# A three-layer transformer on one core: the order of issue found by alternating forward and backward list schedules, and two modulation rows spread by a transpose on TensorE

## The chip, the cores and the metric

The kernel runs on one core of one Trainium2 chip. Its time is the device time of one execution in microseconds (us). The median of the runs is compared before and after the change.

## What is computed

Input is x of 512 tokens by 1024 features, all in float32. A first block has two layers. Each computes a modulation from a condition vector, mixes the tokens, and adds a gated, normalised result:

```python
cond = jax.nn.silu(c)
for layer in range(DEPTH):
    mod = cond @ w_ada[layer] + b_ada[layer]
    shift, scale, gate = jnp.split(mod, 3, axis=-1)
    h = rmsnorm(x, g_pre[layer]) * (1.0 + scale[:, None, :]) + shift[:, None, :]
    ...
    x = x + gate[:, None, :] * rmsnorm(y, g_post[layer])
```

Layer 1's mixer has attention in a sliding window with sinks (8 heads) beside latent attention (8 heads, "MLA"). Layer 2's has differential attention (4 heads) beside forgetting attention (8 heads). In both the concatenated heads are multiplied by `silu` of a gate and go through an output projection w_out. Then follows a second block: one layer with native sparse attention, stick-breaking attention and a gated linear recurrence, an output projection and a layer norm. The output is 512 by 1024.

## The kernel before, in words

**Tiling.** Weights come as tiles of 128 x 1024 float32 (512 KB). Each tile is split into a high part, a rounded copy by ScalarE (L109, `whir<-wrawr`), and a low part, a subtraction on VectorE or POOL (L113, `wlor`). Activations are split likewise (`hh` and `hl`, L90 and L95). A product then takes three matmuls, high by high, high by low and low by high (`mm3`, L80), so that the result is exact to about float32.

**Stages.** The program is written out once, with no loops on the chip. In time: loads and layer 1's first modulation and normalised input (0 to about 62 us), layer 1's input projection and window attention (to about 200), its latent attention (to about 290), the output projection, residual and layer 2's normalised input (to about 350), layer 2 (to about 600), the second block (to about 950) and its output projection with the layer norm.

**Modulation.** `cond @ w_ada` is done on VectorE. Eight tiles of w_ada are loaded (L157, into `graw`, a single buffer; at the start into other free tiles, `V`) and summed up, each times one column of cond: L175 starts and L177 continues the sum `sa`. A matmul with ones over the partitions then makes columns of it (`gemv_cols`, L179 to 186, result `modc`) or a row for the gate (`gate_row`, L205 to 218). Layer 1's rows are needed at once; those of layer 2 and both gates are computed beside layer 1's attention. Layer 1's scaled input is `hh` by ScalarE (L684) and `hl` by VectorE (L690), from `moda` (L682).

**Layer 2's scale and shift** are columns of 128 x 8 and are wanted as rows on all partitions. `spread` (L252 to 258) writes a column to DRAM with its two axes exchanged and reads it back as a row of 1024 on 128 partitions (tag `pth`). The rows are used in `hgen` (L239, L241), which makes layer 2's input of each block of 128 tokens in `residual` (L588 to 623).

**Attention.** Scores `sr` come from TensorE; a custom instruction of VectorE masks them and takes their maximum (L383, `nm`); ScalarE exponentiates (L385); POOL multiplies by the reciprocal sum (L395, `Pr`); TensorE transposes (L140, `tr`); ScalarE and VectorE split the transposed probabilities (`pthr` L90, `ptl` L95); TensorE multiplies by V (`o`). Rotary sums are L316 to L327. The gate's SILU (`gates`, L524 and L526) is one ScalarE instruction over 128 x 2048 between two loads of function tables.

**Order of issue.** All DMAs are issued by SP. Each engine takes its instructions in a fixed order, which a planner (`Plan`, L1784 on) sets when the program is built. It collects dependencies (`edges`): hard ones, ones from the reuse of buffers ("room") and soft ones. `schedule` is a list schedule forward in time over a model of costs (durations, a bus and eight lanes for DMAs, the slower clock of TensorE behind idle time); at each step the engine takes the ready instruction of the lowest rank. The rank is 84% the place in the program and 16% the longest path to the end. `pin` sorts by the modelled start and ties each engine's instructions to that order.

## Time and profile before

| | |
|---|---|
| three runs | 988.75, 992.36, 995.62 us (median 992.36) |
| profiled execution, its own time | 997.87 us |
| its span, first to last instruction | 996.1 us |
| mean granted clock of TensorE | 0.977 |
| busy: TensorE, VectorE, ScalarE, POOL | 919.3, 711.8, 536.0, 245.6 us |
| moved by DMA | 137.38 MB |

TensorE (PE in rows) is busy for 92% of the span, VectorE (DVE) for 71%, ScalarE (ACT) for 54%. A granted clock of 1.00 is 2.4 GHz and 0.50 is 1.2 GHz; TensorE's matmuls then take about twice as long. Busy shares hide which stage an engine waits in, so the profile is to be read by stages and by waits: an idle time in brackets stands behind the instruction that came after it, with what it waited for. PEld is TensorE's weight load.

### The profile page before, as it was taken

The page shows a single profiled execution, that of the slowest core. Times are in us where ns is not written, and L with a number is a line of the kernel's source. Part 1 is how long each engine was busy: PE and PEld are TensorE (multiplying, and loading weights), DVE is VectorE, ACT ScalarE, POOL GpSimd, SP SyncE. Part 2 cuts the span into 40 slices and gives each one's busy share as a digit, 9 for nine tenths or more (in the row PEclk, how much of TensorE's full clock was granted, in tenths as well). Part 3 has the DMA queues.
Part 4 walks back from the last instruction along what each step waited for, and adds up shares of the span by engine and source line. Part 5 has one row for each costly group of instructions (what it writes and reads, how often), then busy time and mean ns, then how long its engine had stood idle before and what let it go on. Part 6 is the DMA issues. An engine that isn't in the chain of part 4 may idle for free.

```text
span 996.1 us, 14786 instructions
## 1 busy us (share of the span) xinstructions
PE 919.3 (92%) x4999; PEld 765.5 (77%) x4999; DVE 711.8 (71%) x1581; ACT 536.0 (54%) x1180; POOL 245.6 (25%) x274
## 2 busy tenths in 40 slices
PE   2899899788799898999999999999999999999996
PEld 1688787666678787879888878986888887888775
DVE  6767768866788954876455856467589788787748
ACT  5543665736654443657345864365254386676820
POOL 1230032202331001322011221014134334544440
PEclk9899999798999999999999999998999999999998
DMA  9637645356565646661454634243422433431142
GB/s 358 258 94 208 206 106 145 101 138 157 160 187 171 199 149 170 174 179 42 124 148 120 189 124 130 87 142 103 135 85 69 106 92 97 128 95 44 49 163 85
DMA packets 56671, 137.38 MB, mean 138 GB/s; under 512 B 15047, under 2 KB 15431, under 8 KB 56596
## 3 DMA queue, kind: packets, MB, share of 16 engines
q1 hardware_dynamic: 56596, 136.44, 46.7%
q8 instruction: 40, 0.66, 0.3%
q14 instruction: 35, 0.29, 0.1%
HBM read 105.42 MB, written 8.44 MB: 114 GB/s over the span
## 4 chain that ended last, share of the span: by engine, by line
PE 44%; DVE 6%; ACT 3%; DMA 2%; issue 1%; POOL 1%; DVEq 0%; ACTq 0%; SPq 0%; POOLq 0%
PE accr L80 32%; PE sr L80 6%; PE o L80 3%; PE tr L140 2%; DMA wrawr<-in_w_out_dram 1%; DVE wlor L113 1%; DMA qk<-qk 1%; DVE ptl L95 1%; PE tr L80 0%; PE sr L140 0%; DMA wrawr<-in_w_dram 0%; ACT whir L109 0%; DVE graw L1660 0%; DVE tmpr L1635 0%; ACT Pr L385 0%
## 5 line engine op out<-in xcount | busy, mean ns | idle before, releaser
L80 PE MATMUL accr<-hh,whir 128*128 128x512 f32 x516 | 208.3, 407 | 5.0 <-DVE qk L327 4.5
L80 PE MATMUL accr<-hl,whir 128*128 128x512 f32 x516 | 208.1, 405 | 4.8 <-DVE hl L690 4.8
L80 PE MATMUL accr<-hh,wlor 128*128 128x512 f32 x516 | 207.3, 405 | 0.0
L109 ACT CAST whir<-wrawr 128x1024 fp32r<-128x1024 f32 (+5 forms) x110 | 111.5, 1014 | 109.4 <-PE accr L80 72.2
L113 DVE TENSOR_TENSOR wlor<-wrawr,whir 128x1024 fp32r<-128x1024 f32 (+6 forms) x93 | 118.3, 1273 | 63.8 <-ACT whir L109 63.5
L395 POOL TENSOR_SCALAR Pr<-Pr,sm 128x256 f32<-128x256 f32 (+2 forms) x120 | 76.8, 656 | 220.9 <-DVE sm L1154 45.8
L80 PEld LDWEIGHTS accr<-hh,whir 128*128 128x128 f32 x516 | 99.0, 192 | 27.9 <-DVE qk L327 5.3
L80 PE MATMUL accr<-whir,hh 128*128 128x256 f32 (+4 forms) x364 | 116.0, 325 | 2.9 <-DVE hS L95 1.0
L385 ACT ACTIVATE Pr<-Pr,nm 128x256 f32<-128x256 f32 (+3 forms) x176 | 95.7, 545 | 41.6 <-DVE nm L383 40.5
L80 PEld LDWEIGHTS accr<-hl,whir 128*128 128x128 f32 x516 | 98.9, 192 | 23.0 <-DVE hl L690 5.7
L80 PE MATMUL accr<-whir,hl 128*128 128x256 f32 (+4 forms) x364 | 115.0, 324 | 0.4 <-DVE hl L95 0.3
L80 PE MATMUL accr<-wlor,hh 128*128 128x256 f32 (+4 forms) x364 | 114.2, 322 | 0.9 <-DVE wlor L113 0.9
L80 PEld LDWEIGHTS accr<-hh,wlor 128*128 128x128 f32 x516 | 98.9, 192 | 20.5 <-issue 1.8
L80 PE MATMUL sr<-qk,qk 128*128 128x256 f32 (+11 forms) x400 | 95.3, 335 | 11.1 <-DVE nm L383 5.1
L95 DVE TENSOR_TENSOR ptl<-tr,pthr 128x256 fp32r<-128x256 f32 (+3 forms) x160 | 72.4, 464 | 25.0 <-ACT pthr L90 21.5
L80 PEld LDWEIGHTS sr<-qk,qk 128*128 128x128 f32 (+2 forms) x400 | 67.5, 196 | 23.9 <-DVE nm L383 10.4
L140 PE MATMUL tr<-ident,Pr 128*128 128x128 f32 x392 | 75.4, 293 | 11.0 <-DVE ptl L95 5.0
L80 PEld LDWEIGHTS accr<-whir,hh 128*128 128x128 f32 x364 | 69.1, 191 | 8.9 <-DVE hS L95 1.2
L80 PEld LDWEIGHTS accr<-whir,hl 128*128 128x128 f32 x364 | 68.8, 190 | 5.4 <-DVE hl L95 0.9
L80 PEld LDWEIGHTS accr<-wlor,hh 128*128 128x128 f32 x364 | 68.8, 191 | 5.1 <-DVE wlor L113 1.2
L140 PEld LDWEIGHTS tr<-ident,Pr 128*128 128x128 f32 x392 | 49.5, 149 | 27.7 <-issue 9.5
L90 ACT CAST pthr<-tr 128x384 fp32r<-128x384 f32 (+3 forms) x124 | 52.9, 439 | 32.5 <-PE tr L140 31.3
(369 smaller groups left out, 1736.5 us busy)
## 6 DMA issues: line engine op xcount, KB each, us to landing
graw<-in_w_ada_dram SPq DMA_DIRECT2D x32, 512.0 KB
wrawr<-in_w_od_dram SPq DMA_DIRECT2D x30, 512.0 KB
wrawr<-in_w_dram SPq DMA_DIRECT2D x29, 512.0 KB
qk<-qk SPq DMA_DIRECT2D x111, 128.0 KB
wrawr<-in_w_out_dram SPq DMA_DIRECT2D x24, 512.0 KB
wrawr<-in_w_ev_dram SPq DMA_DIRECT2D x17, 512.0 KB
V<-in_w_ada_dram SPq DMA_DIRECT2D x14, 512.0 KB
qk<-tmpr SPq DMA_DIRECT2D x34, 128.0 KB
```

Of the source, the lines that this page charges most:

```text
L80: self.nc.tensor.matmul(out, a, b, start=start, stop=stop, skip_group_check=True)
L90: self.nc.scalar.copy(hi, src)
L95: self.nc.vector.tensor_tensor(lo, src, hi.bitcast(F32), ALU.subtract)
L109: self.nc.scalar.copy(hi[:, :n], raw[:, :n])
L113: eng.tensor_tensor(lo[:, :n], raw[:, :n], hi[:, :n].bitcast(F32), ALU.subtract)
L140: self.nc.tensor.transpose(out, in_, self.ident[:k, :k])
L385: nc.scalar.activation(Pi, Pi, AF.Exp, bias=nm[:, i:i + 1], scale=-1.0, accum_out=s[:, i:i + 1])
L395: self.nc.gpsimd.tensor_scalar(v, v, r[:, i:i + 1], 1.0, ALU.mult, ALU.mult)
```

## The change

Two parts. First, the planner searches. `schedule` is split into `graph` (the dependencies in both directions and the longest paths), `forward` (the list schedule as before, which now also returns the modelled end) and a new `backward` (a list schedule from the end, whose times are the latest starts). `pin` does six rounds: forward by a rank, then backward, whose times are the next rank. Of the six forward schedules the one with the earliest modelled end is kept. The first rank takes 10% of the longest path instead of 16%. That DMAs are now known by their type and not by the issuing engine changes nothing, since SP issues them all.

```diff
-    PATH = 0.16
+    PATH, ROUNDS = 0.10, 6
...
+    def backward(self, rank):
+        n = len(self.ins)
+        need = [len(a) for a in self.after]
+        ready, back = [0.0] * n, [0.0] * n
...
+        for _ in range(n):
+            t, e = min((max(free[e], 0.0 if here[e] else coming[e][0][0]), e) for e in range(5) if here[e] or coming[e])
...
+                heapq.heappush(here[e], (-rank[i] - self.cost[i][1], i))
+            i = heapq.heappop(here[e])[1]
+            back[i], free[e] = t, t + self.cost[i][1]
+            for a, kind in self.before[i]:
+                ready[a] = max(ready[a], free[e] - self.cost[a][1] + (0 if kind else self.whole[a] + self.LATENCY[e]))
...
+        return [-b - c[1] for b, c in zip(back, self.cost)]
...
     def pin(self):
         hard, room, soft = self.edges()
-        start = self.schedule(hard, room, soft)
+        path = self.graph(hard, room, soft)
+        n, top = len(path), max(path)
+        rank = [i / n * (1 - self.PATH) - self.PATH * p / top for i, p in enumerate(path)]
+        tries = []
+        for _ in range(self.ROUNDS):
+            tries.append(self.forward(rank))
+            rank = self.backward(tries[-1][1])
+        start = min(tries)[1]
```

Second, `spread` transposes on the chip. TensorE turns the 128 x 8 column into 8 x 128 in PSUM, ScalarE copies it to the row's tile, and the DMA writes eight lines of 512 bytes. It is called twice.

```diff
     def spread(self, col):
         d = self.dram([8, 128])
-        self.nc.sync.dma_start(d.rearrange("c p -> p c"), col)
+        ps = self.p("o")
+        self.tr(ps[0:8, 0:128], col)
         row = self.t([128, 1024], "pth")
+        self.nc.scalar.copy(row[0:8, 0:128], ps[0:8, 0:128])
+        self.nc.sync.dma_start(d, row[0:8, 0:128])
         self.nc.sync.dma_start(row, d.rearrange("(o c) p -> o (c p)", o=1).to_broadcast([128, 1024]))
```

TensorE gets two instructions more and ScalarE two (the copies), and no other engine gains or loses any. Lines from 256 on move down by three. What moves in the order is shown at three places.

VectorE at the start, before: layer 1's first modulation (`modc`, `moda`), the low halves `hl` of its input, and the sum `sa` for its later columns, with tile `V_71` of w_ada.

```order
L177 SCALAR_TENSOR_TENSOR sa_60_258<-V_65_270,cond_5_72,sa_60_258 128x1024
L690 SCALAR_TENSOR_TENSOR hl_59_239<-qk_42_181,moda_57_237,hh_58_238 128x512
L753 TENSOR_SCALAR nsink_87_477<-sink_86_475 128x8
L177 SCALAR_TENSOR_TENSOR sa_60_258<-V_71_308,cond_5_72,sa_60_258 128x1024
L185 TENSOR_TENSOR modc_56_226<-o_55_225,bada_13_94 128x4
L690 SCALAR_TENSOR_TENSOR hl_59_239<-qk_44_188,moda_57_237,hh_58_238 128x512
L682 SCALAR_TENSOR_TENSOR moda_57_237<-modc_56_226,gpre_12_92 128x4
L690 SCALAR_TENSOR_TENSOR hl_59_239<-qk_46_195,moda_57_237,hh_58_238 128x512
L690 SCALAR_TENSOR_TENSOR hl_59_239<-qk_48_202,moda_57_237,hh_58_238 128x512
```

The same place now.

```order
L177 SCALAR_TENSOR_TENSOR sa_60_258<-V_65_270,cond_5_72,sa_60_258 128x1024
L693 SCALAR_TENSOR_TENSOR hl_59_239<-qk_40_174,moda_57_237,hh_58_238 128x512
L693 SCALAR_TENSOR_TENSOR hl_59_239<-qk_42_181,moda_57_237,hh_58_238 128x512
L693 SCALAR_TENSOR_TENSOR hl_59_239<-qk_44_188,moda_57_237,hh_58_238 128x512
L185 TENSOR_TENSOR modc_56_226<-o_55_225,bada_13_94 128x4
L693 SCALAR_TENSOR_TENSOR hl_59_239<-qk_46_195,moda_57_237,hh_58_238 128x512
L685 SCALAR_TENSOR_TENSOR moda_57_237<-modc_56_226,gpre_12_92 128x4
L177 SCALAR_TENSOR_TENSOR sa_60_258<-V_71_308,cond_5_72,sa_60_258 128x1024
L693 SCALAR_TENSOR_TENSOR hl_59_239<-qk_48_202,moda_57_237,hh_58_238 128x512
```

The sum over `V_71` has gone behind two more `hl`, `modc` and `moda`.

ScalarE in layer 1's window attention, before: `Pr2` and `Pr3` are the probabilities of two heads' blocks, `og_233` half of the gate.

```order
L90 CAST pthr0_346_1683<-tr1_351_1699 128x2x128
L385 ACTIVATE Pr2_353_1705,sm_355_1707<-Pr2_353_1705,nm_354_1706 128x128
L524 ACT_TABLE_LOAD
L524 ACTIVATE og_233_1172<-og_233_1172 128x2048
L526 ACT_TABLE_LOAD
L385 ACTIVATE Pr2_353_1705,sm_355_1707<-Pr2_353_1705,nm_354_1706 128x256 x3
L815 ACTIVATE sk_e_360_1728<-nm_354_1706,sink_86_475 128x4
L435 COPY tmpr2_369_1773<-o_368_1764 64x512
L385 ACTIVATE Pr3_376_1798,sm_378_1800<-Pr3_376_1798,nm_377_1799 128x128
L397 ACTIVATE Pr2_353_1705<-Pr2_353_1705,sm_355_1707 128x128
```

The same engine now, some twenty rows later; the exponentials of `Pr2` and `Pr3` stand ahead of the first of these rows.

```order
L854 ACTIVATE hh_363_1741<-accr0_365_1743,subln_362_1739 128x512
L438 COPY tmpr2_369_1773<-o_368_1764 64x512
L90 CAST pthr1_370_1777<-tr0_374_1788 128x2x128
L90 CAST pthr1_370_1777<-tr1_375_1793 128x2x128
L854 ACTIVATE hh_363_1741<-accr1_366_1750,subln_362_1739 128x512
L854 ACTIVATE hh_363_1741<-accr2_367_1757,subln_362_1739 128x512
L854 ACTIVATE hh_363_1741<-accr0_394_1875,subln_362_1739 128x512
L400 ACTIVATE Pr3_376_1798<-Pr3_376_1798,sm_378_1800 128x128
L527 ACT_TABLE_LOAD
L527 ACTIVATE og_233_1172<-og_233_1172 128x2048
L529 ACT_TABLE_LOAD
L90 CAST pthr0_386_1841<-tr0_388_1843 128x128
```

The SILU with its table loads has gone behind the last instruction on `Pr3`.

VectorE in the latent attention, before: `Pr1_541` is a block of scores, `ptl` the low half of transposed probabilities, `graw_518` a tile of w_ada.

```order
L383 ISA Pr1_541_2508,nm_542_2509<-sr1_545_2517,cm_89_481 128x256
L383 ISA nm_542_2509 128x1
L95 TENSOR_TENSOR ptl_506_2366<-tr1_510_2382,pthr1_505_2365 128x4x128
L962 RECIPROCAL sm_513_2391<-sm_513_2391 128x4
L177 SCALAR_TENSOR_TENSOR sa_435_2087<-graw_518_2421,cond_5_72,sa_435_2087 128x1024
L383 ISA Pr1_541_2508,nm_542_2509<-sr0_546_2523,cm_89_481 128x384
L383 ISA nm_542_2509 128x1
L94 CAST pthr0_521_2436<-tr0_523_2438 128x128
```

The same place now.

```order
L386 ISA Pr1_541_2508,nm_542_2509<-sr1_545_2517,cm_89_481 128x256
L386 ISA nm_542_2509 128x1
L439 TENSOR_TENSOR tmpr4_450_2138<-o_503_2352,tmpr2_504_2361 64x512
L965 RECIPROCAL sm_513_2391<-sm_513_2391 128x4
L386 ISA Pr1_541_2508,nm_542_2509<-sr0_546_2523,cm_89_481 128x384
L386 ISA nm_542_2509 128x1
L95 TENSOR_TENSOR ptl_506_2366<-tr0_509_2376,pthr1_505_2365 128x3x128
L95 TENSOR_TENSOR ptl_506_2366<-tr1_510_2382,pthr1_505_2365 128x4x128
L94 CAST pthr0_521_2436<-tr0_523_2438 128x128
L386 ISA Pr1_541_2508,nm_542_2509<-sr1_547_2529,cm_89_481 128x512
```

The sum over `graw_518` is gone from here and stands 43 rows later; those over `graw_502`, `graw_548`, `graw_564` and `graw_581` have moved back by 35, 42, 38 and 31 rows. On SP the two writes of `spread` stood in layer 1's attention, 95 and 62 rows ahead of their reads; now both writes and both reads stand within five rows, behind the last load of w_out0.

## Rows read from the trace of the kernel before

**Rows 1.** Stages: length; busy us (instructions) of PE, PEld, DVE, ACT, POOL; PEclk; DMA; GB/s.

```profile
0.00:62.00 62.00, 36.48 (x194) 30.33 (x194) 43.97 (x72) 34.52 (x59) 11.83 (x10) 0.94 0.65 248
...
200.00:232.00 32.00, 25.90 (x120) 20.21 (x119) 18.04 (x42) 10.93 (x24) 1.05 (x1) 0.95 0.57 135
232.00:290.00 58.00, 49.25 (x274) 40.10 (x275) 48.67 (x131) 41.90 (x111) 21.22 (x27) 0.94 0.60 166
...
450.00:700.00 250.00, 249.95 (x1312) 209.42 (x1311) 149.18 (x308) 138.66 (x278) 48.08 (x53) 0.99 0.42 123
```

**Rows 2.** TensorE's waits: tile, line, releaser: us in total, times, longest.

```profile
PE sr L140 <- DMA ident<-in_ident_dram: 19.6, 1, 19.6
PE sr L80 <- DVE nm L383: 5.1, 4, 3.3
PE tr L140 <- DVE ptl L95: 5.0, 6, 1.9
...
PE accr L80 <- DVE hl L690: 4.8, 1, 4.8
PE accr L80 <- DVE qk L327: 4.5, 2, 2.9
PE sr L140 <- DVE Pr L241: 4.5, 2, 3.4
```

**Rows 3.** Granted clock in four slow stretches and in the last projection.

```profile
35.20:42.00 6.80, 5.74 (x14) 4.48 (x15) 6.31 (x11) 4.55 (x6) 2.05 (x1) 0.50 0.52 190
...
188.80:195.60 6.80, 6.24 (x27) 5.18 (x27) 5.21 (x11) 4.37 (x13) 2.90 (x5) 0.50 0.27 78
226.30:229.70 3.40, 3.40 (x10) 2.73 (x11) 0.00 (x0) 0.00 (x0) 0.00 (x0) 0.50 0.45 107
243.40:246.80 3.40, 3.16 (x13) 2.61 (x12) 2.83 (x12) 2.72 (x8) 0.43 (x1) 0.50 0.56 116
...
965.55:987.62 22.07, 22.03 (x97) 17.70 (x95) 18.13 (x39) 2.55 (x7) 2.39 (x1) 1.00 0.13 49
```

**Rows 4.** VectorE's timeline at the start: start, duration, line, operation, operands.

```profile
32.38 3.10 DVE L177 SCALAR_TENSOR_TENSOR sa<-V,cond,sa 128x1024 f32<-128x1024 f32 x1 [1.58 <-DMA V<-in_w_ada_dram]
...
36.20 0.74 DVE L690 SCALAR_TENSOR_TENSOR hl<-qk,moda,hh 128x512 fp32r<-128x512 f32 x1
```

**Rows 5.** ScalarE's timeline about the gate's SILU in layer 1.

```profile
179.41 1.28 ACT L524 ACT_TABLE_LOAD   x1
...
183.92 0.51 ACT L385 ACTIVATE Pr<-Pr,nm 128x256 f32<-128x256 f32 x1
```

**Rows 6.** TensorE's timeline behind it; in brackets the idle time before and its releaser.

```profile
187.19 0.55 PE L140 MATMUL tr<-ident,Pr 128*128 128x128 f32 x3 [2.60 <-POOL Pr L395]
```

**Rows 7.** SP's timeline: a w_ada row, the column's write, a later w_ada row.

```profile
207.47 0.33 SPq L157 DMA_DIRECT2D graw<-in_w_ada_dram  x1
208.74 0.38 SPq L255 DMA_DIRECT2D d<-moda  x1
...
236.75 0.58 SPq L157 DMA_DIRECT2D graw<-in_w_ada_dram  x1
```

**Rows 8.** VectorE's timeline: three sums over w_ada rows.

```profile
217.57 1.28 DVE L177 SCALAR_TENSOR_TENSOR sa<-graw,cond,sa 128x1024 f32<-128x1024 f32 x1 [2.86 <-DMA graw<-in_w_ada_dram]
...
241.43 1.28 DVE L177 SCALAR_TENSOR_TENSOR sa<-graw,cond,sa 128x1024 f32<-128x1024 f32 x1 [0.85 <-DMA graw<-in_w_ada_dram]
...
258.18 1.28 DVE L177 SCALAR_TENSOR_TENSOR sa<-graw,cond,sa 128x1024 f32<-128x1024 f32 x1 [3.77 <-DMA graw<-in_w_ada_dram]
```

**Rows 9.** DMA packets from 212 to 219 us.

```profile
DMA packets 503, 0.34 MB, mean 48 GB/s; under 512 B 414, under 2 KB 414, under 8 KB 503
```

**Rows 10.** ScalarE's timeline: the cast of a chunk of w_out0.

```profile
223.19 1.04 ACT L109 CAST whir<-wrawr 128x1024 fp32r<-128x1024 f32 x1 [5.99 <-DMA wrawr<-in_w_out_dram]
```

**Rows 11.** Instructions on the spread rows: durations, first and last start.

```profile
L257 SPq DMA_DIRECT2D pthr<-d x2: 327/327/327, 286.3 to 293.2; - x2
...
L239 DVE SCALAR_TENSOR_TENSOR Pr<-Pr,st_r,pthr x8: 742/748/753, 319.4 to 344.9; 128x512 f32<-128x512 f32 x8
```

More of the change, by code (lines that the diff above doesn't have):

```diff
@@ L1801, in __init__ @@
                      if hasattr(getattr(getattr(a, "bass_ap", None), "tensor", None), "tag_meta")] for x in self.ins]
+        self.dma = [type(x).__name__ == "InstDMACopy" for x in self.ins]
         self.cost = [self.duration(x, e) for x, e in zip(self.ins, self.eng)]
@@ L1895, in edges @@
                     if (w or w2) and j != i and p0 < q1 and q0 < p1 and (m is m2 or (m & m2).any()):
-                        same = self.eng[j] == self.eng[i] < 4
+                        same = self.eng[j] == self.eng[i] and not self.dma[i] and not self.dma[j]
                         (soft if same and (not w2 or self.eng[i] == 0) else hard).add((j, i))
@@ L1926, in edges, with graph @@
         return hard, room, {e for e in soft - hard if e[0] != e[1]}
-    def schedule(self, hard, room, soft):
+    def graph(self, hard, room, soft):
         n = len(self.ins)
-        after = [[] for _ in range(n)]
-        need = [0] * n
+        after, before = ([[] for _ in range(n)] for _ in range(2))
         for s, kind in ((hard | {(v, f) for u, f in room for v in u}, 0), (soft, 1)):
@@ L1935, in schedule @@
                 after[a].append((b, kind))
-                need[b] += 1
-        path, left = [0.0] * n, list(need)
+                before[b].append((a, kind))
+        self.after, self.before = after, before
+        self.whole = [d + occ + act / self.BYTES_PER_NS if q else d for (d, occ, act), q in zip(self.cost, self.dma)]
+        path, left = [0.0] * n, [len(b) for b in before]
         order = [i for i in range(n) if not left[i]]
@@ L1945, in schedule, with forward @@
         for i in reversed(order):
-            d, occ, act = self.cost[i]
-            if self.eng[i] == 4:
-                d += act / self.BYTES_PER_NS + occ
-            path[i] = max([d] + [path[j] + (occ if k else d + 35) for j, k in after[i]])
-        top = max(path)
-        rank = [i / n * (1 - self.PATH) - self.PATH * path[i] / top for i in range(n)]
-        for i, x in enumerate(self.ins):
-            if type(x).__name__ == "InstLoadActFuncSet":
-                rank[i] = -2.0
+            path[i] = max([self.whole[i]] + [path[j] + (self.cost[i][1] if k else self.whole[i] + 35) for j, k in after[i]])
+        return path
+    def backward(self, rank):
+        n = len(self.ins)
+        need = [len(a) for a in self.after]
+        ready, back = [0.0] * n, [0.0] * n
+        free = [0.0] * 5
+        coming, here = [[] for _ in range(5)], [[] for _ in range(5)]
+        for i in range(n):
+            if not need[i]:
+                heapq.heappush(coming[self.eng[i]], (0.0, i))
+        for _ in range(n):
+            t, e = min((max(free[e], 0.0 if here[e] else coming[e][0][0]), e) for e in range(5) if here[e] or coming[e])
+            while coming[e] and coming[e][0][0] <= t:
+                i = heapq.heappop(coming[e])[1]
+                heapq.heappush(here[e], (-rank[i] - self.cost[i][1], i))
[3 more added lines that the diff above has]
+                ready[a] = max(ready[a], free[e] - self.cost[a][1] + (0 if kind else self.whole[a] + self.LATENCY[e]))
+                need[a] -= 1
+                if not need[a]:
+                    heapq.heappush(coming[self.eng[a]], (ready[a], a))
+        return [-b - c[1] for b, c in zip(back, self.cost)]
+    def forward(self, rank):
+        n = len(self.ins)
+        after, need, last = self.after, [len(b) for b in self.before], 0.0
+        rank = [-1e9 if type(x).__name__ == "InstLoadActFuncSet" else r for x, r in zip(self.ins, rank)]
         ready, start = [0.0] * n, [0.0] * n
@@ L1999, in schedule @@
                     a = b
-            elif e == 4:
+            elif self.dma[i]:
                 t = max(t, lanes.popleft())
@@ L2004, in schedule @@
                 lanes.append(end)
-            start[i], free[e] = t, t + occ
+            start[i], free[e], last = t, t + occ, max(last, end)
             for j, kind in after[i]:
@@ L2012, in schedule @@
                     heapq.heappush(coming[f], (ready[j], j))
-        return start
+        return last, start
     def pin(self):
         hard, room, soft = self.edges()
-        start = self.schedule(hard, room, soft)
+        path = self.graph(hard, room, soft)
[6 more added lines that the diff above has]
+        start = min(tries)[1]
         order = sorted(range(len(self.ins)), key=lambda i: start[i])
```

## Prediction, made before the changed kernel ran

> **What bounds the kernel now.** I read the trace from the whole to the single wait. First the busy time cut into stages [rows 1]: from 450 to 700 us TensorE is busy for 249.95 of 250 us, so nothing is to be won there by a better order. The idle time lies early: 25.5 us in the first 62, 6.1 between 200 and 232, 8.8 between 232 and 290, to name three stages. Second, what TensorE waited for [rows 2]: 19.6 of the first 25.5 us are the wait for the identity matrix at the very start, which no order of the other engines removes. The other five rows name VectorE, 23.9 us together, each time for a single tile that came late (nm, ptl, hl, qk, Pr). Third, the granted clock [rows 3]: behind most of these waits it stands at 0.50, 1.2 GHz, for 3.4 or 6.8 us. At full clock 97 matmuls of 512 columns took 22.03 us, 227 ns each; in the stretch from 35.2 us 14 took 5.74 us, 410 ns each. So a wait is paid up to one and a half times. Last, the timelines of the engines named, to see why they were late: in nearly every case an instruction for which a DMA had not landed, or a long one, stands at the head of a queue, ahead of the short one that TensorE needed. So the time early in the kernel is set by order of issue, and the change is one of order. Median runs took 992.36 us; the profiled one 997.87 us with a span of 996.1. Terms are worked out on the profiled run.
>
> **A, the start.** VectorE's modulation sum takes a row of w_ada that lands late: L177 starts at 32.38 us and lasts 3.10, and the halves hl that feed the first matmuls come behind it, at 36.20 [rows 4]. TensorE waits 4.8 us for hl [rows 2] and then runs 6.8 us at half clock, which costs 14 x (410 - 227) = 2.6 us. In the new order three more hl and modc stand ahead of that L177. Against it, the identity is issued behind one more load of 512 KB; at the 248 GB/s of the stage [rows 1] that is 2.1 us at most. Bounds: -7.4 and +2.1. I take -5, that is -7.4 with the later start, since hl and the row had their inputs.
>
> **B, the gate's SILU.** ScalarE does a table load, a SILU over 128x2048 and a table load, 179.41 to 183.92 us, ahead of the exponentials of the attention in progress [rows 5]; TensorE then waits 2.60 us for that attention's probabilities, which POOL normalises behind them [rows 6], and the clock is at half from 188.8 to 195.6. The new order puts the block behind these exponentials, and the matmuls for the gate, off the path, among the attention's. The wait of 2.60 and half of the 6.8 us at half clock [rows 3], 3.4, make 6.0. If the SILU comes late instead, its consumer waits the same 4.5 us. Bounds -6.0 and +4.5; I take -4.5, since SILU's result is needed only for the products with the attention's output, much later.
> The row gives 1.28 us for a table load [rows 5]. The Trainium skill (ScalarE: Activation LUTs, "What ACT_TABLE_LOAD costs") counts a drain beside the load, 2.66 us per switch in all; by that the block would be an estimated 2 x 2.66 us and the SILU's 1.95 (4.51 - 2 x 1.28), 7.3 us, and the term 2.8 us larger. The trace does not agree: 4.51 us lie between the first load's start and the next exponential's.
>
> **C, the writes of four bytes.** Today the two modulation columns (128 x 8) are written to DRAM transposed, 1024 packets of four bytes each, during layer 1. The second is issued at 208.74, just behind a w_ada row at 207.47 [rows 7]. That row's user on VectorE starts only at 217.57, 10.1 us after its issue [rows 8], where the one issued at 236.75 was used at 241.43, 4.7 us after. The window of the transfers says why [rows 9]: 414 of its 503 packets are under 512 B, and 48 GB/s are moved where the stage's mean is 135 [rows 1]. Two waits of TensorE hang on it: for qk behind that L177, and again for qk behind ScalarE's cast of a w_out0 chunk that waited 5.99 us [rows 10]; together 4.5 us [rows 2], and 3.4 us at half clock from 226.3 [rows 3], worth 1.7: 6.2 us. The change transposes the column on TensorE, copies 8x128 on ScalarE (no row shows that copy; the exponential of 128x256 took 0.51 us [rows 5], so between 0 and 0.5 each) and writes eight lines of 512 bytes, about 295 us, when the columns have long been ready. Three transposes of 128x128 took TensorE 0.55 us [rows 6]; two smaller ones, among the dense products of layer 1's output, add 0.4 at the most. The new order also sends that L177 ahead of two weight halves and three rotary sums; with the row landed 4.7 us after issue, at 212.2, it holds nobody, with 10.1 it holds TensorE some 3 us more. Bounds -6.2 and +3; I take -4.5, as the other rows of w_ada land in about 4.7.
> The Trainium skill says (DMA: Bandwidth & Descriptors, "Specifications" and "Rules for kernel authors") that under 512 B a transfer costs a read-modify-write and that a strided last dimension makes one descriptor per element. The trace agrees in what follows such a write, 48 GB/s in [rows 9]; that it is the write, and not the load it shares the time with, no row shows. By the rule the full 6.2 us would go; were it not so, C would be the order's part alone, near zero.
>
> **D, the latent heads.** L177 waits for a w_ada row at the head of VectorE's queue ahead of the softmax's low halves, at 241.43 and 258.18 and once between them (0.85 to 3.77 us of idle time each) [rows 8]. TensorE waits 1.9 and 3.3 us for ptl and nm behind these two, the longest of each in [rows 2], and for the third about as long as for the first: 7.1. Half clock follows twice, from 243.4 for 3.4 us [rows 3] and once more alike, worth 3.4. Together 10.5. In the new order five of these L177 stand 31 to 43 places later, where their rows have landed. What is late next: the gate row, used near 297 us, now ends its sum just ahead of it; if it is late, each load of 4.7 us that is still ahead of it comes back, one or two of them. Bounds -10.5 and 0; I take -7.5, a little nearer to the full sum less one half-clock stretch, 8.8, than to one such load given back, 5.8.
>
> **E, the residual and layer 2's first transposes.** TensorE waits 4.5 us in two waits for Pr of L241 [rows 2], and a stretch at half clock as above, 1.7, follows. VectorE did weight halves and an L177 before L241; now L241 comes first, but the two broadcast reads, issued at 286.3 and 293.2 [rows 11], now follow their writes at once, which takes them past three loads of w_out0 and one of w_ada on SP, an estimated 3 to 8 us later; first use is at L239 from 319.4 [rows 11], so at least 18 us of cover stand for read and landing. Bounds -6.2 and +3, the weight halves' price if TensorE then waits for them; I take -2.5, between the two, as the halves put behind are TensorE's too.
>
> **F, the rest.** From 350 on, shifts are of one to three us and TensorE is full; I take -1, bounds -4 and +4. SP issues as many DMAs as before, of the same sizes bar the two columns.
>
> Sum: -5 - 4.5 - 4.5 - 7.5 - 2.5 - 1 = -25. From 997.87 that is 972.9 for a profiled run; from the median 992.36, 967.4. I predict **968 us**.
>
> **The rivals.**
> *Given back (within 1%).* TensorE reaches 450 us earlier but waits there for weights: SP issues every DMA in order, and w_ada and w_out chunks share its buffers. For it: the first 62 us already move 248 GB/s [rows 1], and rows of w_ada sit in one buffer. Against: between 450 and 700 TensorE never waits, so the loads are ahead there. It would leave A's and half of C's gain, about -7: 985 us.
> *Slower.* VectorE's queue is blocked at the new places. L177 for two rows stands ahead of rotary sums near 213 us, and five stand close together between 267 and 296, each with its load begun only when the single buffer is free. If a load takes 10.1 us as once above, instead of 4.7, seven instructions each hold the queue 5.4 us; TensorE pays this and up to 1.7 us of half clock at, say, five of them: 35 us against gains elsewhere of 20, so +15: 1007 us. It decides from a landing time of about 8 us. Against it: the row without such a write ahead landed in 4.7 us [rows 7, 8].
> *Larger.* Every bound on the gaining side holds: -7.4 - 6 - 6.2 - 10.5 - 6.2 - 4 = -40: 952 us.
> *The change doesn't do what it says.* The rounds keep an order near the old one. The moves shown speak against it; it would give the time of before, less C: 987 us.
>
> **How the numbers follow.** Forecast (-12 to -34 us) 0.62; larger 0.12; given back or not done 0.18 (0.14 and 0.04); slower 0.08. One per cent, 10 us, is about what a measurement of this kernel tells from no change, as its three runs spread over 7 us. Faster by over 1%: 0.62 + 0.12 + a small part of the given-back case, 0.03, = 0.77; within 1% 0.15; slower by over 1% 0.08. Range 950 to 990: from the larger case to the given-back one with the bounds of the unknowns; the forecast's own is 958 to 980.
>
> **What would show it.** A: TensorE's wait at 31 us for hl gone and the clock at 1.00 behind it. B: no table load between exponentials near 180 us. C: no load of a w_ada row with a use 8 us or more behind its issue near 144 and 208, and no cast waiting 6 us for w_out0. D: no VectorE idle time before L177 while latent heads run. E: the wait for Pr of L241 below 2 us. Wrong, if TensorE's idle time before 350 us stays above 50 us, or if it falls by 20 us and the span does not, with new idle time behind 350 us.

## The result, and the profile after

The changed kernel's median is 958.77 us (958.08 to 961.73, four runs), that of the kernel before 993.99 (988.75 to 997.09, four runs). The ratio is 0.9657, with a 95% interval from 0.9608 to 0.9705, so the change takes off about 34 us; 25 were forecast (968 us), and 958.77 lies in the stated range. The profiled execution spans 957.6 us instead of 996.1, at a mean granted clock of 0.987 instead of 0.977.

The stages of the changed kernel, columns and windows as in [rows 1]:

```profile
0.00:62.00 62.00, 40.24 (x221) 35.28 (x222) 48.93 (x80) 35.65 (x60) 12.85 (x10) 1.00 0.71 264
...
200.00:232.00 32.00, 29.59 (x145) 24.36 (x144) 21.56 (x67) 20.93 (x58) 6.64 (x11) 0.84 0.67 170
232.00:290.00 58.00, 55.30 (x282) 44.85 (x281) 53.27 (x105) 37.88 (x91) 19.20 (x19) 0.97 0.59 184
...
450.00:700.00 250.00, 249.74 (x1298) 209.76 (x1297) 154.42 (x305) 133.55 (x266) 45.95 (x56) 1.00 0.46 134
```

The idle time of TensorE in the first 62 us fell from 25.5 to 21.8, which is now the wait for the identity alone; from 200 to 232 it fell from 6.1 to 2.4, from 232 to 290 from 8.8 to 2.7. The stretch from 450 to 700 is as full as it was. A window of the changed kernel holds later work than the same window before, so the table below goes by work.

TensorE's waits, as in [rows 2]:

```profile
PE sr L140 <- DMA ident<-in_ident_dram: 21.8, 1, 21.8
PE sr L80 <- DMA qk<-qk: 2.6, 1, 2.6
PE accr L80 <- DVE V L606: 2.6, 1, 2.6
PE accr L80 <- DVE V L95: 1.8, 2, 1.6
PE sr L80 <- DMA qk<-hh: 1.7, 1, 1.7
PE tr L140 <- DVE ptl L95: 1.5, 3, 1.0
```

Of the five waits for VectorE in [rows 2] (nm, ptl, hl, qk, Pr; 23.9 us) only that for ptl is still above 1 us in all, with 1.5 instead of 5.0. The identity comes 2.2 us later, as A had it. TensorE's idle time before 350 us, for which the forecast named 50 us as a sign of being wrong, is 34.6 us instead of 57.0. New are two waits for V and one for a copy by DMA of the latent heads' inputs (`qk<-hh`). The V of L606 is the product with the gate row, of which D says more below. The copy has consequences. TensorE's timeline at the two waits near 200 us, and VectorE's ahead of the first:

```profile
196.55 0.47 PE L80 MATMUL accr<-hh,whir 128*128 128x512 f32 x1 [1.57 <-DVE V L95]
...
207.25 0.47 PE L80 MATMUL sr<-qk,qk 96*128 96x128 f32 x2 [1.65 <-DMA qk<-hh]
```

```profile
194.78 1.28 DVE L177 SCALAR_TENSOR_TENSOR sa<-graw,cond,sa 128x1024 f32<-128x1024 f32 x1 [2.01 <-DMA graw<-in_w_ada_dram]
```

The sum over a w_ada row, now ahead of V's low half, waits 2.0 us for its load, which was issued at 188.90, 5.9 us earlier. SP issues loads and copies in one order and stands at the next load of the single buffer until this sum is done, to 196.1; the first copy goes out at 197.6, and TensorE waits 1.65 us for one of them. That the late load is what delays the copies is read from this order; no run separates it.

The granted clock, as in [rows 3], in every slow stretch but that of the last 7 us:

```profile
177.70:181.10 3.40, 3.16 (x16) 2.83 (x15) 3.37 (x6) 1.42 (x5) 0.00 (x0) 0.50 0.04 7
208.40:218.70 10.30, 9.94 (x31) 8.33 (x30) 5.97 (x23) 7.16 (x21) 2.29 (x5) 0.50 0.62 144
276.70:280.10 3.40, 3.11 (x7) 2.48 (x8) 3.40 (x9) 0.85 (x1) 0.00 (x0) 0.50 0.63 172
358.60:362.00 3.40, 3.07 (x9) 2.67 (x10) 0.73 (x4) 0.55 (x3) 0.00 (x0) 0.50 0.55 128
```

The clock stands at half for 20.5 us in these four; before, it did so for 41 us in nine. The longest now, 10.3 us from 208.4, begins a microsecond behind the wait for `qk<-hh`.

To put the gain in its places, I count TensorE's work: each matmul with its columns divided by 2400, in us, plus 0.016, and at least 0.11 (what the trace shows where none waits); the kernel has 876 us of it. The table gives the time at which a share of it was done.

| work done, us | before, at us | after, at us | gained so far | in this step | what lies there |
|---|---|---|---|---|---|
| 20 | 51.8 | 47.3 | 4.5 | 4.5 | A, the start |
| 80 | 112.0 | 106.6 | 5.4 | 0.9 | |
| 100 | 136.7 | 126.6 | 10.1 | 4.7 | first probabilities of the window attention |
| 160 | 211.9 | 193.2 | 18.8 | 8.7 | B, the gate's SILU |
| 180 | 240.4 | 222.7 | 17.7 | -1.1 | C, the second column write |
| 200 | 273.9 | 243.6 | 30.3 | 12.6 | D, latent heads, first part |
| 240 | 316.0 | 289.0 | 27.0 | -3.3 | D, to the residual |
| 260 | 340.8 | 309.8 | 31.0 | 4.0 | E, the residual |
| end | 996.1 | 957.6 | 38.5 | 7.5 | F, the rest |

So 31 of the 38.5 us lie ahead of 341 us. The rows of the residual say the same with no counting: L612, now L615, starts first at 285.1 instead of 311.8, and L239, whose row answers to [rows 11], at 291.1 instead of 319.4.

```profile
L615 DVE TENSOR_TENSOR tmpr<-accr,V x8: 679/681/692, 285.1 to 595.6; 128x512 f32<-128x512 f32 x8
...
L239 DVE SCALAR_TENSOR_TENSOR Pr<-Pr,st_r,pthr x8: 744/746/749, 291.1 to 313.5; 128x512 f32<-128x512 f32 x8
```

The table, though, compares one profile with one profile. Five profiles with the same order of every engine up to 140 us (before, e1, e4, e6, e7) reach 20 us of work between 49.7 and 51.8, and 100 us of work between 132.8 and 136.9; a step of 2 to 4 us in the table is therefore no evidence by itself.

### The profile page after: what moved, and what is told of

It is laid out like the page before. It is cut to its first block, busy times and chain, and to the rows that moved or that the text cites. A ratio compares the mean times of both kernels' runs of the same rounds, so it can differ in the third digit from the quotient of the medians.

```text
span 957.6 us, 14806 instructions
## 1 busy us (share of the span) xinstructions
PE 908.6 (95%) x5001; PEld 764.1 (80%) x5001; DVE 707.7 (74%) x1581; ACT 535.0 (56%) x1182; POOL 243.7 (25%) x274
## 3 DMA queue, kind: packets, MB, share of 16 engines
q1 hardware_dynamic: 54548, 136.44, 47.3%
## 4 chain that ended last, share of the span: by engine, by line
PE 68%; DVE 12%; DMA 11%; ACT 4%; issue 3%; SPq 2%; POOL 0%; DVEq 0%; ACTq 0%; POOLq 0%
PE accr L80 46%; PE sr L80 10%; PE o L80 6%; PE tr L140 4%; DMA qk<-qk 2%; DMA tmpr<-tmpr 2%; DMA wrawr<-in_w_ev_dram 1%; DVE wlor L113 1%; DMA wrawr<-in_w_out_dram 1%; DMA graw<-in_w_ada_dram 1%; DMA ident<-in_ident_dram 1%; DMA og<-in_w_ada_dram 1%; PE sr L140 1%; SPq L370 1%; DMA qk<-tmpr 1%
## 5 line engine op out<-in xcount | busy, mean ns | idle before, releaser
L109 ACT CAST whir<-wrawr 128x1024 fp32r<-128x1024 f32 (+4 forms) x110 | 111.3, 1013 | 105.8 <-PE accr L80 65.7
L113 DVE TENSOR_TENSOR wlor<-wrawr,whir 128x1024 fp32r<-128x1024 f32 (+7 forms) x93 | 111.5, 1202 | 69.6 <-ACT whir L109 69.1
L140 PE MATMUL tr<-ident,Pr 128*128 128x128 f32 x392 | 68.4, 282 | 1.9 <-DVE ptl L95 1.5
L386 DVE CUSTOM_DVE_ANT_0 Pr<-sr,cm 128x128 f32<-128x128 f32 (+3 forms) x96 | 45.0, 484 | 25.7 <-PE sr L80 25.2
```

The source lines that it names most:

```text
L109: self.nc.scalar.copy(hi[:, :n], raw[:, :n])
L113: eng.tensor_tensor(lo[:, :n], raw[:, :n], hi[:, :n].bitcast(F32), ALU.subtract)
L140: self.nc.tensor.transpose(out, in_, self.ident[:k, :k])
L386: nc.vector.tensor_tensor_reduce(out=Pi, in0=ps[:, :N], in1=add(i), op0=ALU.add, op1=ALU.min, scale=-c, scalar=1e38 if init is None else i ...
```

## The experiments

Ratios are to runs of the kernel before on the same chip, with 95% intervals. The changed kernel's is 0.9657, on another.

### The new spread alone, the new order alone

**e1_spread_only**, the old planner:

```diff
-        self.nc.sync.dma_start(d.rearrange("c p -> p c"), col)
+        ps = self.p("o")
+        self.tr(ps[0:8, 0:128], col)
...
+        self.nc.scalar.copy(row[0:8, 0:128], ps[0:8, 0:128])
+        self.nc.sync.dma_start(d, row[0:8, 0:128])
```

> The kernel before with the new spread alone (transpose on TensorE, lines of 512 bytes); the planner is the old one and its order stays nearly word for word. Theory 'the four-byte writes clog the transfers behind them': the w_ada row issued at about 207 us is used some 5 us later instead of 10, TensorE's two waits for qk near 218 and 223 us (4.5 us) and the half-clock stretch from 226 (worth 1.7) go, and the time falls by 4 to 7 us. Rival 'the load was late for the traffic it shared the time with': the two waits stay within 1 us of what they were and the time stays within 2 us of before.

988.22 us, ratio 0.9909 (0.9873 to 0.9945): 9 us, above the 4 to 7 expected. By the count of work 6.0 of them are won between 160 and 170, where the two waits for qk had been. The row issued at 203.37 is used 7.4 us later, not 5, but VectorE does not wait for it. The theory of the clogging write holds.

**e2_rounds_only**, the new planner with the old write:

```diff
-        self.tr(ps[0:8, 0:128], col)
...
-        self.nc.sync.dma_start(d, row[0:8, 0:128])
+        self.nc.sync.dma_start(d.rearrange("c p -> p c"), col)
```

> The changed kernel with the old spread (writes of four bytes). Theory 'the new order earns nearly all of the gain': 27 to 34 us faster than before. Theory 'the four-byte writes clog': 4 to 8 us slower than the changed kernel, with loads of w_ada used 8 us or more behind their issue near the two writes. Rival: within 2 us of the changed kernel.

978.58 us, ratio 0.9815 (0.9777 to 0.9852): 18 us faster than before, and by the ratios 16 slower than the changed kernel, twice what was expected at most. Its order is not that of the changed kernel: for the other write the planner finds another one, in which some 650 of TensorE's 5001 instructions and 360 of VectorE's 1581 stand elsewhere. So the 16 us are the write and another order together. SP's timeline of this kernel, the two column writes and the loads of w_ada beside them, and VectorE's, where these rows are used:

```profile
136.76 0.39 SPq L255 DMA_DIRECT2D d<-modc  x1
137.75 0.34 SPq L157 DMA_DIRECT2D graw<-in_w_ada_dram  x1
...
205.47 0.33 SPq L157 DMA_DIRECT2D graw<-in_w_ada_dram  x1
207.62 0.38 SPq L255 DMA_DIRECT2D d<-moda  x1
```

```profile
150.78 1.28 DVE L177 SCALAR_TENSOR_TENSOR sa<-graw,cond,sa 128x1024 f32<-128x1024 f32 x1 [7.33 <-DMA graw<-in_w_ada_dram]
...
217.53 1.28 DVE L177 SCALAR_TENSOR_TENSOR sa<-graw,cond,sa 128x1024 f32<-128x1024 f32 x1 [5.76 <-DMA graw<-in_w_ada_dram]
```

The rows are used 13.0 and 12.1 us behind their issue, and VectorE sits idle for 7.3 and 5.8 us in front of them; TensorE then waits 5.96 us for ptl and 5.48 us for qk. By the count of work the kernel loses some 8 us to the changed one in each of these two places. Before, the rows beside the two writes were used 8.7 and 10.1 us behind their issue, with 1.0 and 2.9 us of idle time. So in this order a write costs more than in the old one, in part because the rows land later still, in part because less slack lies in front of VectorE. The two parts of the change, 9 and 18 us alone, make 34 together.

**e4_plain_write**, the kernel before with lines of 32 bytes:

```diff
-        d = self.dram([8, 128])
-        self.nc.sync.dma_start(d.rearrange("c p -> p c"), col)
+        d = self.dram([128, 8])
+        self.nc.sync.dma_start(d, col)
```

> The kernel before with only the two column writes changed from 1024 packets of four bytes to 128 lines of 32 bytes, at the same places of the same order on every engine; the transposition is left out, so layer 2's scale and shift stand in another order of features. Theory 'the four-byte writes clog': the row issued at 207 us is used some 5 to 7 us behind its issue, the two waits for qk near 220 us fall by 3 us or more, and the time falls by 3 to 6 us. Rival 'shared traffic' or 'any write in small pieces': within 2 us of before.

991.33 us, ratio 0.9936 (0.9903 to 0.9969): 6 us. Every engine's order is that of before, so nothing but the write's packets differs. SP's and VectorE's rows at the second write, to be held against [rows 7] and [rows 8]:

```profile
206.30 0.33 SPq L157 DMA_DIRECT2D graw<-in_w_ada_dram  x1
207.57 0.33 SPq L255 DMA_DIRECT2D d<-moda  x1
```

```profile
213.26 1.27 DVE L177 SCALAR_TENSOR_TENSOR sa<-graw,cond,sa 128x1024 f32<-128x1024 f32 x1
```

7.0 us from issue to use instead of 10.1, and no idle time for the row at all instead of 2.86. By the count of work 5.6 us are won between 160 and 170, and what follows adds up to nothing. [rows 9] needs a closer look: its small packets are over by 213.2, and then no packet starts until 214.7. What is slow is the traffic behind them. These are the packets of the six microseconds from 214.5 before, and of those from 213.0 in e4:

```profile
DMA packets 129, 0.40 MB, mean 66 GB/s; under 512 B 13, under 2 KB 13, under 8 KB 129
```

```profile
DMA packets 518, 1.15 MB, mean 191 GB/s; under 512 B 93, under 2 KB 93, under 8 KB 517
```

In the first window hardly a small packet is left, and yet only a third of the bytes of the second are moved. As the two runs differ in the write alone, the four-byte write slows the 4 KB packets of the next load, a chunk of w_out0.

### Which part of the planner

**e3_one_round**:

```diff
-    PATH, ROUNDS = 0.10, 6
+    PATH, ROUNDS = 0.10, 1
```

> The changed kernel with one round instead of six: a single forward schedule by the first rank, with 10% of the longest path instead of 16. Theory 'the alternation finds the order': at most a third of the gain, so 5 to 12 us faster than before. Rival 'the other weight of the path does it': within 5 us of the changed kernel, 30 us faster than before.

988.59 us, ratio 0.9911 (0.9881 to 0.9941), as the new spread alone (0.9909). The other weight of the path gives nothing that can be measured; the alternation gives 0.9911 to 0.9657, 25 us, as its theory had it.

**e12_two_rounds**, the same line with 2:

> The changed kernel with two rounds instead of six: forward, backward, forward. Theory 'one pass from the end brings most of it': within 6 us of the changed kernel, 0.965 to 0.972 of before. Rival 'it takes the later rounds': 0.978 or more.

969.49 us, ratio 0.9735 (0.9690 to 0.9780): in between the two. One pass from the end brings 18 of the 25 us, the later rounds about 8.

**e9_pe_ranks** and **e10_rest_ranks**: a last forward schedule with ranks from two sources. In e10 the condition is `!= 0`; engine 0 is TensorE.

```diff
+        rank = min(tries)[2]
+        own = [i / n * (1 - 0.16) - 0.16 * p / top for i, p in enumerate(path)]
+        start = self.forward([rank[k] if self.eng[k] == 0 else own[k] for k in range(n)])[1]
```

> The changed kernel, but a last forward schedule in which only TensorE ranks its instructions by the alternation's latest starts; the four other engines rank as before the change (84% program order, 16% longest path). Theory P 'the gain is TensorE's own order: independent products placed into the waits of a softmax': two thirds of what the alternation adds to the spread (0.991 to 0.966), so 0.975 or less of before. Rival Q 'the gain lies in the order of those who feed TensorE': 0.985 or more. Third, 'only both together': within 3 us of the spread alone, 0.988 to 0.994, here and in e10.

> The reverse: VectorE, ScalarE, POOL and SP rank by the alternation's latest starts, TensorE as before the change. Theory P: 0.985 or more of before. Rival Q: 0.975 or less. Third, 'only both together': 0.988 to 0.994.

980.74 us, ratio 0.9838 (0.9796 to 0.9879), and 980.80, ratio 0.9841 (0.9796 to 0.9886). Neither theory holds: each half of the ranks brings about 7 us beyond the spread alone (0.991; their intervals overlap its own a little) and both together 25, so some 11 come only when TensorE and those who feed it are ordered for each other. TensorE's timeline at the start, first of e9, then of e10:

```profile
31.57 1.22 PE L80 MATMUL accr<-hh,whir 128*128 128x512 f32 x2 [1.45 <-ACT whir L109]
```

```profile
31.70 1.22 PE L80 MATMUL accr<-hh,whir 128*128 128x512 f32 x2 [1.02 <-ACT hh L687]
34.11 0.79 PE L80 MATMUL accr<-hl,whir 128*128 128x512 f32 x1 [1.20 <-DVE hl L693]
```

With TensorE's ranks alone the wait for hl is gone: TensorE takes two products of high parts in turn and waits 1.45 us once. With the others' ranks alone it still waits for hl, though less (1.20). The first has done 20 us of work at 47.0, as early as the changed kernel (47.3), the second at 50.2, as late as the spread alone (49.8). So at the start the gain goes with TensorE's ranks. But the schedule is a joint one: in e9 VectorE, too, does three hl from 29.75 to 31.81, two of which come at 32.52 and 35.27 in the spread alone.

### Single moves

The next three are the old order with the new spread, in which one thing goes to its place in the new order. The planner makes both orders and moves the listed instructions behind their predecessors in the new one:

```diff
+        move = set(self.moves())
+        for e in range(5):
+            lists[e] = [k for k in lists[e] if k not in move]
+            for p, k in enumerate(aim[e]):
+                if k in move:
+                    lists[e].insert(lists[e].index(aim[e][p - 1]) + 1, k)
```

**e5_start_move** (the sum over V_71, instruction 176):

> The kernel before with the new spread (which alone took 0.991 of the time of before) and one instruction moved: at the start, VectorE's sum over the late w_ada row (tile V_71) goes behind modc, one more hl and moda, as in the new order; every other instruction stays where it was. Theory A: the wait of 4.8 us for hl goes and some of the half clock behind it, 4 to 7 us less than the spread alone, near 0.985 of before. Rival: the sum, now later, is missed at once, and the time stays within 2 us of the spread alone.

985.51 us, ratio 0.9897 (0.9865 to 0.9930), no different from the spread alone. TensorE's timeline, beside the one wait of 3.75 us for hl that the spread alone shows at 35.33:

```profile
35.68 0.50 PE L80 MATMUL accr<-hh,wlor 128*128 128x512 f32 x1 [2.42 <-POOL wlor L113]
...
39.66 0.80 PE L80 MATMUL accr<-hl,whir 128*128 128x512 f32 x1 [0.84 <-DVE hl L693]
```

The wait for hl has become one of 2.42 for POOL's low half of the weights and one of 0.84 for the next hl. What was late next is just as late. The edit also puts one more hl ahead of the sum, where the new order has two.

What takes the time back stands in POOL's timeline. These are its half of a weight before, the same in e5, the hl of VectorE beside it in e5, and POOL's half in the changed kernel:

```profile
32.06 2.34 POOL L113 TENSOR_TENSOR wlor<-wrawr,whir 128x1024 fp32r<-128x1024 f32 x1 [7.67 <-ACT whir L109]
```

```profile
32.36 3.26 POOL L113 TENSOR_TENSOR wlor<-wrawr,whir 128x1024 fp32r<-128x1024 f32 x1 [7.72 <-ACT whir L109]
...
33.33 7.60 DVE L693 SCALAR_TENSOR_TENSOR hl<-qk,moda,hh 128x512 fp32r<-128x512 f32 x5
```

```profile
26.26 2.97 POOL L113 TENSOR_TENSOR wlor<-wrawr,whir 128x1024 fp32r<-128x1024 f32 x1 [1.34 <-ACT whir L109]
```

A sum or an hl of VectorE that starts while POOL does its half takes some 2 us longer. Before, this was the sum itself: it took 3.10 us [rows 4], where the next sum, at 39.79, took 1.28. In the spread alone, in the same order, the sum came 1.1 us earlier and kept its 1.28; an hl then took 2.76, and TensorE waited 3.75 us for hl all the same. In e5 the sum passes ahead of POOL in 1.28 us, and two of the five hl take 2.84 and 2.85 us instead of 0.74, the second beside another half of POOL's at 36.48. In the changed kernel POOL's half comes 5.8 us earlier, beside a sum that takes 3.26 us, and POOL does nothing more until 38.10, so that the hl take 0.7 us each.

**e6_silu_move** (the SILU and the table load behind it, 1263 and 1264):

> The kernel before with the new spread and one block moved: in layer 1's window attention ScalarE's table load, SILU and table load go behind the last instruction on the probabilities of that pair, as in the new order; all else stays. Theory B: TensorE's wait of 2.6 us for these probabilities goes and part of the half clock, 3 to 6 us less than the spread alone, near 0.987 of before. Rival: TensorE has nothing else placed there, so the wait only moves; within 1.5 us of the spread alone.

991.09 us, ratio 0.9951 (0.9927 to 0.9976): not faster, rather slower than the spread alone. TensorE's and ScalarE's timelines:

```profile
185.70 0.55 PE L140 MATMUL tr<-ident,Pr 128*128 128x128 f32 x3 [2.30 <-POOL Pr L398]
...
197.00 1.09 PE L140 MATMUL tr<-ident,Pr 128*128 128x128 f32 x4 [3.95 <-DVE ptl L95]
```

```profile
189.50 1.28 ACT L527 ACT_TABLE_LOAD   x1
190.79 1.91 ACT L527 ACTIVATE og<-og 128x2048 f32<-128x2048 f32 x1
192.71 1.28 ACT L529 ACT_TABLE_LOAD   x1
```

The wait for Pr stays, 2.30 us instead of 2.59: the SILU was not its only cause. Behind the exponentials VectorE adds up and inverts their sums, before POOL can normalise. This is VectorE's addition before the change, then ScalarE's last instruction on the sums and the same addition in e6:

```profile
185.73 0.16 DVE L816 TENSOR_TENSOR sm<-sm,sk_e 128x4 f32<-128x4 f32 x1 [0.20 <-ACT sk_e L815]
```

```profile
182.00 0.28 ACT L818 ACTIVATE sk_e<-nm,sink 128x4 f32<-128x4 f32 x1
...
184.25 0.16 DVE L819 TENSOR_TENSOR sm<-sm,sk_e 128x4 f32<-128x4 f32 x1
```

Before, VectorE waited only 0.20 us for ScalarE. In e6 ScalarE is done at 182.28, and VectorE comes to the addition at 184.25, behind the masks of the next pair and the low half of a weight. VectorE's queue was as late as ScalarE's. And the SILU, now behind the pair, holds up the next casts on ScalarE, and TensorE waits 3.95 us for ptl.

**e7_sum_moves** (the five sums of the latent heads and the loads of their single buffer):

> The kernel before with the new spread, and in the latent heads VectorE's five sums over w_ada rows moved to their places in the new order (31 to 43 rows later), their loads on SP following as the single buffer comes free; all else stays. Theory D: the three waits for ptl and nm go with the two half-clock stretches, 6 to 10 us less than the spread alone, near 0.983 of before. Rival: the gate's row is then late for the residual, and the time stays within 2 us of the spread alone.

990.28 us, ratio 0.9930 (0.9902 to 0.9959): no gain over the spread alone. TensorE's timeline:

```profile
235.87 0.52 PE L140 MATMUL tr<-ident,Pr 128*128 128x128 f32 x3 [2.32 <-DVE ptl L95]
...
256.93 0.66 PE L140 MATMUL tr<-ident,Pr 128*128 128x128 f32 x4 [1.75 <-DVE ptl L95]
...
272.69 0.66 PE L140 MATMUL tr<-ident,Pr 128*128 128x128 f32 x4 [1.02 <-DVE ptl L95]
...
280.60 0.66 PE L140 MATMUL tr<-ident,Pr 128*128 128x128 f32 x4 [0.73 <-DVE ptl L95]
```

By the count of work it gains 3.9 us on the spread alone between 180 and 190 and loses 5.6 between 190 and 220. The first wait for ptl, 2.54 us in the spread alone, stays at 2.32; where the sums now stand, new waits for ptl of 1.75, 1.02 and 0.73 us appear.

### Trying for more

**e8_ident_first**:

```diff
+        for k in range(n):
+            if self.dma[k] and any(w and t.name.startswith("ident") for w, t, *_ in self.acc[k]):
+                rank[k] = -1e9
```

> The changed kernel with the identity matrix loaded first of all, which the planner is told by the lowest rank; it plans the rest around that. Theory 'the start is set by the identity': TensorE transposes x from about 8 us on instead of 21.8, and the time falls by 4 to 8 us below the changed kernel, to 0.958 to 0.962 of before. Rival 'the start is set by the sum of w_ada rows on VectorE': the first product still begins near 30 us, and the time stays within 2 us of the changed kernel, 0.964 to 0.968 of before.

962.65 us, ratio 0.9672 (0.9638 to 0.9706): the rival. TensorE's timeline:

```profile
9.83 0.47 PE L140 MATMUL sr<-ident,Pr 128*128 128x128 f32 x1 [9.83 <-ACT Pr L671]
...
30.09 1.22 PE L80 MATMUL accr<-hh,whir 128*128 128x512 f32 x2 [1.08 <-ACT hh L687]
```

The transposes begin at 9.83 instead of 21.8, but the first product at 30.09; in the changed kernel it begins at 31.57. That the sum over w_ada rows sets it is what the rival says; the run shows that the identity does not. And with its early work spread out TensorE now runs at half clock from 29.7 to 36.5 us, where the changed kernel ran at full.

**e11_dma_price**:

```diff
-    BYTES_PER_NS, DMA_LATENCY, LANES = 410.0, (1700.0, 2300.0), 8
+    BYTES_PER_NS, DMA_LATENCY, LANES = 410.0, (2600.0, 3300.0), 8
-    PATH, ROUNDS = 0.10, 6
+    PATH, ROUNDS = 0.10, 12
```

> The changed kernel, its planner told that a DMA lands 0.9 to 1.0 us later (2.6 and 3.3 us beside the bytes instead of 1.7 and 2.3), near the 4.5 us from issue to use that the traces show for a row of 512 KB, with twelve rounds. Theory 'what is left of the early waits comes from loads that the plan believes landed': the waits for qk behind a DMA (1.7 and 2.6 us) and the half clock behind them go, 3 to 8 us below the changed kernel, 0.958 to 0.963 of before. Rival 'the price does not decide': 0.964 to 0.970.

957.96 us, ratio 0.9607 (0.9568 to 0.9645). Its interval overlaps the changed kernel's (0.9608 to 0.9705), so 0.5% is probable and not shown, and price and number of rounds were changed together. TensorE's waits:

```profile
PE tr L140 <- DVE ptl L95: 4.2, 5, 1.5
PE sr L80 <- DMA qk<-qk: 1.9, 2, 1.5
PE accr L80 <- DVE qk L330: 1.8, 2, 0.9
```

The wait for `qk<-hh` is gone and that for `qk<-qk` fell from 2.6 to 1.9 in two; waits for VectorE took their place, that for ptl 4.2 us instead of 1.5.

## Why the prediction was right, and where its steps were not

The direction, the range and the place (ahead of 350 us) were right; the size was 25 against 34. That the sum came this near is in part luck: the three moves that the forecast prices in A, B and D gain nothing alone (e5, e6, e7), C failed in its place, and gains that the sum does not hold made up for it. What was right is that the early time is set by the order of issue; that the order had to change on all engines at once the forecast did not say. The general rule that a wait is paid up to one and a half times does not fit the forecast's own B, 2.60 us of waiting and 6.0 in all. Step by step, by the table of work:

**A, -5; measured -5.4 by 112 us.** The size is less sure than it looks: e1 and e4, with the order of before at the start, are 2.0 and 2.1 us ahead of the profile of before at 20 us of work. The cause was half right. It was forecast from three hl ahead of the sum, where the orders show two, and from a sum that lasts 3.10 us; of these 1.8 us are the time beside POOL's weight half. e5 made most of the move alone and gained nothing, since POOL's halves then fell on the hl. The new order has the hl earlier, POOL's half away from them and TensorE on other products; e9 puts this gain down to TensorE's ranks, and no run moves POOL's half alone.

**B, -4.5; measured -8.7.** The step "TensorE then waits 2.60 us for that attention's probabilities, which POOL normalises behind them" had the cause wrong: e6 moved the block and the wait stayed, with VectorE's queue as late as ScalarE's. The 8.7 also hold a wait that the forecast did not count, 1.82 us at 177.45 for a copy by DMA (`qk<-tmpr`), with half clock from 178.5 to 181.9 behind it. The stage was sped up by the order of all engines together: between 100 and 160 us of work e9 gains 3.5 us on the spread alone, e10 2.0, and the changed kernel 9.0.

**C, -4.5; measured +1.1 in its place.** The mechanism, loads held up by the four-byte write, is shown by e1 and e4; e2 agrees. The forecast had said that no row shows whether the write is to blame; e4 shows it, as with lines of 32 bytes most of the loss is gone. Of the two rules of the Trainium skill that the forecast cites (DMA: Bandwidth & Descriptors, "Specifications" and "Rules for kernel authors"), this speaks for the second, one descriptor per element: 1024 packets became 128. The first, the limit of 512 bytes, is not what cost most here, since 32 bytes are far under it. What failed is "it holds nobody": the row for the sum at 194.78 us came 5.9 us behind its issue, not 4.7, and was waited for 2.0 us, and then the latent heads' copies by DMA were late. These 1.65 us, and 10.3 us at half clock behind them, worth about 5, took the place of the waits removed. And the write's price was put at 6.2 us at most; alone it was 9 (e1, from 5.5 to 12.7), and in the order of e2 more, in two places. The first write, at 143 us, was seen and not priced. The two copies on ScalarE took 0.26 us each.

**D, -7.5; measured -9.3 (-12.6 and +3.3).** The size was near, the cause not shown: the sums moved alone returned what they gained (e7), in new waits for ptl and not at the gate row. Between 180 and 200 us of work each half of the ranks alone brings most of it: e9 gains 7.5 us there on the spread alone, e10 8.8, the changed kernel 10.7. In the changed kernel it is the gate row that gives the +3.3 back, as the forecast had feared:

```profile
276.99 0.79 PE L80 MATMUL accr<-whir,qk 128*128 128x512 f32 x1 [2.56 <-DVE V L606]
```

The last sum ends at 268.5, POOL finishes the row (L217) at 275.8, VectorE multiplies with it (L606) from 276.3, and TensorE, which waited 2.56 us, stands at half clock from 276.7 to 280.1.

**E, -2.5; measured -4.0.** Right in sign; the wait for Pr of L241, 4.5 us in [rows 2], is down to 0.7. The late rows cost nothing: L239 starts at 291.1, and no wait for them shows.

**F, -1; measured -7.5.** "TensorE is full" held from 450 to 700 us alone and hid a half-clock stretch from 690.5 to 697.3, worth up to 3.4 us and gone now. Between 700 and 850 us TensorE was idle for 4.3 us and is for 1.7, and by the count of work about 4 us are won behind 700. That the slow stretch went with the change is not shown; e4, with the order of before, kept it (684.7 to 691.5), and e1, nearly the same order, had none.

**Not in the sum: -4.7 between 112 and 137 us.** Before, TensorE waits there for the window attention's first probabilities (the other of the two waits for POOL's Pr; the one in [rows 6] is 2.60), and the clock is at half from 123.9 to 127.3. Both are gone, and the forecast has no term for them. That they went with the change is not shown: e1, with the order of before up to there, waits 1.66 us, has no slow stretch there and is 3.9 us ahead of before at 100 us of work.

The rival "slower" did occur in miniature, at 195 and 207 us, without deciding. The rival "larger" forecast 952 as the sum of all bounds; the measured kernel came close, with C missing and F above its bound.

## What to carry to other kernels

When a trace shows an instruction that holds up a queue, ask what is late just behind it, and whether it is long only beside another engine, before pricing the wait: three such moves, made alone, gave nothing, while a schedule that ranks every engine by latest starts gave 25 us. Rows of four bytes written by DMA are to be priced by the loads behind them, not by their own 4 KB; in the one other order tried the price was higher. The greedy list schedule here gained most from one pass from the end; the weight of the longest path in its rank gave nothing.

## What the runs showed of the hardware

**A small write slows what stands beside and behind it.** Beside 1024 packets of four bytes a 512 KB load was used 8.7 and 10.1 us behind its issue (before), and 13.0 and 12.1 (e2), where another took 4.7; with the same 4 KB in 128 lines of 32 bytes it was 7.0, without a wait. The small packets of the second write were over by 213.2 us; for the six microseconds from 214.5 the traffic behind them moved at 66 GB/s, against 191 in e4.

**VectorE and POOL get in each other's way.** An hl of 128x512 takes VectorE 0.74 us, and 2.76 where it starts while POOL subtracts a weight half (e1, 32.52); a sum over 128x1024 takes 1.28, and 3.10 there (before). Where the sum started first (e5, 32.13), it kept its 1.28 us, and POOL's half took 3.26 instead of 2.36.

**The clock's slow stretch at one place is not always the same length.** Before and e4 have the same order up to the first column write at 143 us. The trace of before waits 4.83 us for hl and stands at half clock from 35.2 to 42.0 us; e4's waits 3.55 and stands there from 36.1 to 39.5, and at 20 us of work e4 is 2.1 us ahead. At 100 us of work five profiles of that order lie 4.1 us apart. A difference of that size between two profiles at one place is thus no evidence by itself; the ratios over runs are.
